# FFN up projection: four pairs of chunks by Strassen's algorithm, with sums of weight quarters made by accumulating DMA transfers

## The chip, the cores and the metric

The kernel runs on one NeuronCore of a Trainium2 chip. The engines are TensorE (PE: matmuls, into PSUM banks), VectorE (DVE), ScalarE (ACT), GpSimd (POOL) and SyncE (SP), which issues most DMA transfers. Each engine works through its own queue in order; 16 DMA engines serve all the queues that issue transfers. The metric is the time of one execution on the device in microseconds (us), as the median of several runs.

## The reference

Two layers of a decoder trunk over 256 tokens and 1024 channels, all in float32. Each layer has two half-step FFNs, one before and one after a mixer of three kinds of attention, and then a gated input embedding:

```python
def swiglu(x, w1, w3, w2):
    return (jax.nn.silu(x @ w1) * (x @ w3)) @ w2
...
    for i in range(DEPTH):
        h = h + 0.5 * swiglu(rms_norm(h, g_ffn1[i]), w1_a[i], w3_a[i], w2_a[i])
        u = rms_norm(h, g_mix[i])
        h = h + hybrid_mixer(u, w_in[i], ...)
        h = h + 0.5 * swiglu(rms_norm(h, g_ffn2[i]), w1_b[i], w3_b[i], w2_b[i])
        ple_gate = jax.nn.sigmoid(rms_norm(h, g_ple[i]) @ w_ple_gate[i])
        h = h + ple_gate * (p[i] @ w_ple_proj[i])
    return rms_norm(h, g_final)
```

The change touches only the FFNs, of which there are four. The hidden width is 2816.

## The kernel before

**Precision.** TensorE multiplies in the format fp32r. To keep float32 accuracy each operand is split into a rounded part `hi` (a cast on ScalarE) and a remainder `lo` (a subtraction on VectorE), and each product is three matmuls (`mm3`, lines 101 to 104: hi x hi, hi x lo, lo x hi). One such matmul has a 128x128 stationary part and a 128x512 moving part, which is the weights.

**Chunks of the up projection.** The hidden width is cut into 11 chunks of 256. A chunk has 512 columns: 256 of `w1` and 256 of `w3`. The 1024 rows of its weights come in four units of 128x1024 (512 KB each). A plain chunk is, for two blocks of 128 tokens and eight blocks of 128 rows, three matmuls each: 2 x 8 x 3 = 48. A plain unit (`up_unit`, line 222) loads one of the four units (`load`, line 75: a transfer on SP's queue, a cast, a remainder) and gives 12 matmuls. `gated` (line 234) makes silu(a) * b from the result, `turn` (243) transposes it with four TensorE transposes and splits it, and `down_unit` (260) loads 512 KB of `w2` and adds 12 matmuls to four PSUM banks that hold the down projection.

**Pairs.** Two chunks together are a product of 2 x 2 blocks: token blocks by halves of the rows for x, halves of the rows by chunks for the weights. Strassen's algorithm, in Winograd's form, makes it with seven products of 12 matmuls instead of eight, 84 instead of 96 for two chunks. Each product takes a sum or a quarter of the weights and a sum or a quarter of x. `x_forms` (267) makes those of x once per FFN. `winograd` (311) fetches the eight units of a pair's quarters; `form` (323) makes four sums of quarters on VectorE, two units each (line 320); `make` (335) splits the two units that a product needs, into the buffers `whi` and `wlo`, of which there are seven each for all weights; `products` (348) issues the seven products and the sums of their results. The matmuls of two products that follow one another may add to one bank, with a copy or sum taken out of it between.

**Order.** Per FFN the chunks 0 to 6 are plain and (7, 8) and (9, 10) are pairs. Chunks 0 to 2 come first. Then `block` (line 384) runs a pair: eight steps, each with the splits for the next product, a product, a plain unit of chunks 3 to 6, and a down unit. What the code says is not yet the order on the engines: the framework's planner simulates the program with assumed durations when it is built, reorders the instructions of each engine by that, and puts in the semaphore waits. After that each queue is fixed. The last chunks' down units, the residual sum into `h` and the next norm end the FFN.

Of the kernel before, what the change touches and what calls it, by code (L numbers as in the profile page):

```python
# [14 lines left out]
P = 128  # L15
# [18 lines left out]
def trunk(ctx: ExitStack, tc: tile.TileContext, a: dict, out: bass.AP):  # L34
# [77 lines left out]
    def bank_tr():  # L112
        return bank("tr", 2)
# [77 lines left out]
    def ffn(li, w13, w2, r, g, first=False, aside=None):  # L191
        nonlocal ident
        with tc.tile_pool(name=nm("fp"), bufs=3) as fp:

            def wtile():
                return fp.tile([P, U], F32, tag="wr", name=nm("wr"), bufs=10)

            def t512(name):
                return fp.tile([P, 512], F32, tag="t512", name=nm(name), bufs=4)
# [67 lines left out]
            def x_forms():  # L267
# [31 lines left out]
                V.tensor_tensor(out=s1, in0=a10, in1=a11, op=ALU.add)  # L299
# [5 lines left out]
                sub(a01, a01, s1)  # L305
# [5 lines left out]
            def winograd(c, fx):  # L311
                ws, t2s, fw = [], [], {}
                for u in range(2):
                    ws.append({(kh, nh): wtile() for kh in range(2) for nh in range(2)})
                for kh, nh in ((0, 0), (1, 0), (0, 1), (1, 1)):
                    for u in range(2):
                        nc.sync.dma_start(ws[u][kh, nh], w13[li, c + nh, 2 * kh + u])

                def sub(out, a, b):
                    V.tensor_tensor(out=out, in0=a, in1=b, op=ALU.subtract)  # L320
# [23 lines left out]
                def add(out, a, b):  # L344
                    V.tensor_tensor(out=out, in0=a, in1=b, op=ALU.add)


                def products():
                    o = bank_tr()
# [7 lines left out]
                    o = bank_tr()  # L357
                    product(o, 6, True)
                    u2 = t512("u2")
                    add(u2, o, m1)  # L360
# [758 lines left out]
```

## Time and profile before

| | us |
|---|---|
| median of 3 runs (lowest, highest) | 1333.01 (1332.68, 1333.23) |
| the profiled execution: its time | 1332.86 |
| its span in the trace | 1331.1 |
| TensorE busy, in the span | 1312.2 |
| VectorE / ScalarE busy | 994.0 / 802.8 |
| second FFN (first layer), about | 448 to 634 |

The page's first part gives busy time and share of the span by engine, the second 40 equal slices, the fourth the chain of work that ended last. A row of a group reads: line, engine, operation, output <- inputs, shapes, count | busy us, mean ns of one | idle time of the engine before these instructions, and which instruction ended it. `whi<-raw` and `wlo<-raw` are the two halves of a split of a plain load, `whi<-wr` and `wlo<-wr` those of a pair's unit; `wr<-wr,wr` are the sums of quarters; `tr`, `mm` and `acc` are PSUM banks. A row of the timeline gives start, duration and count. A row of the view of stretches gives the stretch, its length, busy time (and instructions) of each engine, TensorE's granted clock, the mean busy share of the DMA engines, and GB/s.

### The profile page before, as it was taken

How to read it: one execution, taken by the hardware profiler on the slowest of the kernel's cores; microseconds unless marked ns; L12 is line 12 of the kernel's file. 1: busy time of each engine (PE TensorE's matmuls, PEld its weight loads, DVE VectorE, ACT ScalarE, POOL GpSimd, SP SyncE). 2: the span in 40 equal slices, each digit the busy share in tenths (PEclk: the TensorE clock that was granted, in tenths of full speed). 3: DMA queues.
4: the chain of work that ended last, by engine and by line, in shares of the span. 5: the costliest groups of instructions: out<-in, count | busy, mean ns of one | idle time of the engine just before them, and what ended most of it. 6: DMA issues, size and time to landing. Idle time of an engine off the chain costs nothing.

```text
span 1331.1 us, 17969 instructions
## 1 busy us (share of the span) xinstructions
PE 1312.2 (99%) x6624; PEld 1097.5 (82%) x6624; DVE 994.0 (75%) x1414; ACT 802.8 (60%) x1205; POOL 50.2 (4%) x109
## 2 busy tenths in 40 slices
PE   9999999999999999999999999999999999999997
PEld 7788879978888888887888888898888788888876
DVE  7998755666768789975789986566676677999755
ACT  6665546665775655654756665466667835655645
POOL 1000000001100000000100000000010000000001
PEclk9999999999999999999999999999999999999999
DMA  8774537534455567455566646373444465583542
GB/s 296 274 269 127 187 103 228 171 123 132 147 169 175 161 227 276 122 164 182 163 239 196 217 128 210 103 224 127 159 142 143 144 204 167 206 299 102 180 145 80
DMA packets 67769, 236.63 MB, mean 178 GB/s; under 512 B 8160, under 2 KB 8800, under 8 KB 67680
## 3 DMA queue, kind: packets, MB, share of 16 engines
q1 hardware_dynamic: 67104, 234.39, 54.0%
q8 instruction: 52, 0.85, 0.3%
q10 hardware_dynamic: 576, 1.08, 0.2%
q14 instruction: 37, 0.30, 0.1%
HBM read 234.40 MB, written 1.05 MB: 177 GB/s over the span
## 4 chain that ended last, share of the span: by engine, by line
PE 94%; ACT 2%; DVE 2%; DMA 1%; issue 1%; POOL 0%; SPq 0%; POOLq 0%; ACTq 0%; DVEq 0%
PE mm L102 17%; PE mm L104 17%; PE mm L103 17%; PE acc L102 8%; PE acc L103 8%; PE acc L104 8%; PE tr L104 4%; PE tr L102 4%; PE tr L103 4%; PE tr L250 1%; PE tr L150 1%; ACT whi L86 1%; PE tr L716 1%; DVE wlo L87 1%; DMA h<-in_x 1%
## 5 line engine op out<-in xcount | busy, mean ns | idle before, releaser
L87 DVE TENSOR_TENSOR wlo<-raw,whi 128x1024 fp32r<-128x1024 f32 (+1 forms) x378 | 450.1, 1201 | 137.3 <-ACT whi L86 135.1
L86 ACT CAST whi<-raw 128x1024 fp32r<-128x1024 f32 (+1 forms) x378 | 387.3, 1035 | 198.2 <-PE mm L104 77.5
L102 PE MATMUL mm<-whi,xhi 128*128 128x512 f32 (+1 forms) x760 | 296.0, 393 | 0.0
L103 PE MATMUL mm<-wlo,xhi 128*128 128x512 f32 (+1 forms) x760 | 295.1, 389 | 0.3 <-DVE wlo L87 0.3
L104 PE MATMUL mm<-whi,xlo 128*128 128x512 f32 (+1 forms) x760 | 295.2, 389 | 0.0
L102 PEld LDWEIGHTS mm<-whi,xhi 128*128 128x128 f32 x760 | 143.0, 188 | 30.0 <-DVE sqk L516 0.7
L104 PEld LDWEIGHTS mm<-whi,xlo 128*128 128x128 f32 x760 | 142.8, 188 | 29.7 <-DVE xlo L136 0.7
L103 PEld LDWEIGHTS mm<-wlo,xhi 128*128 128x128 f32 x760 | 142.9, 188 | 28.9 <-DVE wlo L87 0.8
L135 ACT CAST whi<-wr 128x1024 fp32r<-128x1024 f32 (+1 forms) x120 | 121.6, 1023 | 66.9 <-PE acc L104 38.9
L136 DVE TENSOR_TENSOR wlo<-wr,whi 128x1024 fp32r<-128x1024 f32 (+1 forms) x120 | 140.6, 1185 | 24.8 <-ACT whi L135 23.6
L102 PE MATMUL acc<-whi,fhi 128*128 128x512 f32 x352 | 132.0, 393 | 7.7 <-ACT fhi L135 7.7
L103 PE MATMUL acc<-wlo,fhi 128*128 128x512 f32 x352 | 137.9, 392 | 0.4 <-DVE wlo L87 0.4
L104 PE MATMUL acc<-whi,flo 128*128 128x512 f32 x352 | 134.6, 390 | 0.0
L102 PEld LDWEIGHTS acc<-whi,fhi 128*128 128x128 f32 x352 | 65.7, 188 | 23.2 <-ACT fhi L135 9.6
L103 PEld LDWEIGHTS acc<-wlo,fhi 128*128 128x128 f32 x352 | 66.1, 188 | 15.2 <-DVE wlo L87 1.8
L104 PEld LDWEIGHTS acc<-whi,flo 128*128 128x128 f32 x352 | 66.1, 188 | 13.6
L320 DVE TENSOR_TENSOR wr<-wr,wr 128x1024 f32<-128x1024 f32 x64 | 76.3, 1217 | 0.0
L102 PE MATMUL mm<-xhi,whi 128*128 128x256 f32 x256 | 73.8, 288 | 0.0
L104 PE MATMUL mm<-xhi,wlo 128*128 128x256 f32 x256 | 72.5, 283 | 0.0
L103 PE MATMUL mm<-xlo,whi 128*128 128x256 f32 x256 | 72.4, 283 | 0.0
L102 PE MATMUL tr<-whi,q 128*128 128x512 f32 x160 | 63.7, 398 | 0.0
L104 PE MATMUL tr<-whi,q 128*128 128x512 f32 x160 | 62.6, 391 | 0.0
(248 smaller groups left out, 1960.8 us busy)
## 6 DMA issues: line engine op xcount, KB each, us to landing
raw<-in_w13b SPq DMA_DIRECT2D x56, 512.0 KB, 3.7
raw<-in_w13a SPq DMA_DIRECT2D x52, 512.0 KB, 4.2
raw<-in_wg SPq DMA_DIRECT2D x48, 512.0 KB, 3.7
raw<-in_w2a SPq DMA_DIRECT2D x44, 512.0 KB, 4.4
raw<-in_w2b SPq DMA_DIRECT2D x44, 512.0 KB, 4.3
wr<-in_w13a SPq DMA_DIRECT2D x32, 512.0 KB, 6.7
raw<-in_wqk SPq DMA_DIRECT2D x32, 512.0 KB, 4.1
wr<-in_w13b SPq DMA_DIRECT2D x32, 512.0 KB, 6.2
```

The lines of the kernel that those rows point to most:

```text
L86: A.copy(hi[:, c], raw[:, c])
L87: V.tensor_tensor(out=lo[:, c], in0=raw[:, c], in1=hi[:, c].bitcast(F32), op=ALU.subtract)
L102: PE.matmul(o, lhs[0], rhs[0], start=first, stop=False, **more)
L103: PE.matmul(o, lhs[0], rhs[1], start=False, stop=False, **more)
L104: PE.matmul(o, lhs[1], rhs[0], start=False, stop=last, **more)
L135: A.copy(hi, t)
L136: V.tensor_tensor(out=lo, in0=t, in1=hi.bitcast(F32), op=ALU.subtract)
L150: PE.transpose(t[:, j * P : (j + 1) * P], h[tb][:, k * P : (k + 1) * P], ident)
L250: PE.transpose(t[:, j * S + tb * P : j * S + (tb + 1) * P], prs[c, tb][:, j * P : (j + 1) * P], ident)
L320: V.tensor_tensor(out=out, in0=a, in1=b, op=ALU.subtract)
L716: PE.transpose(t[:, j * P : (j + 1) * P], e[:, j * P : (j + 1) * P], ident)
```

## The change

Chunks 0 to 2 stay plain, and (3, 4), (5, 6), (7, 8) and (9, 10) are pairs. A pair has four tiles x, y, w and z of two units each. The sums of quarters are no longer made on VectorE: with the signs of x's forms changed, every sum of the weights is a running sum of quarters, and `plus` adds a further quarter to a tile in SBUF by a DMA transfer with `accum_op=add`, issued from POOL's queue, after the tile's last split. Tile w is b01 + b00 for product 5, then + b11 for product 6, then + b10 for product 4; tile z is b11 for product 3, then + b01 for product 7. The products run in the order 1, 2, 5, 3, 6, 7, 4. The results of 5 and 3 are copied out by ScalarE and combined later. The order of products (S), plain units (P), down units (D) and transposes (T) stands in four plans; the quarters of the next pair are fetched one tile at a time from the third S on, and the three later pairs use the other two PSUM banks (`mm`).

```diff
             def wtile():
-                return fp.tile([P, U], F32, tag="wr", name=nm("wr"), bufs=10)
+                return fp.tile([P, U], F32, tag="wr", name=nm("wr"), bufs=12)

             def t512(name):
-                return fp.tile([P, 512], F32, tag="t512", name=nm(name), bufs=4)
+                return fp.tile([P, 512], F32, tag="t512", name=nm(name), bufs=5)
...
-                V.tensor_tensor(out=s1, in0=a10, in1=a11, op=ALU.add)
+                sub(s1, a10, a11)
...
-                sub(a01, a01, s1)
+                V.tensor_tensor(out=a01, in0=a01, in1=s1, op=ALU.add)
...
-            def winograd(c, fx):
...
-                for kh, nh in ((0, 0), (1, 0), (0, 1), (1, 1)):
+            ORDER = (1, 2, 5, 3, 6, 7, 4)
+
+            def pair(c, bank):
+                def at(kh, nh, u):
+                    return w13[li, c + nh, 2 * kh + u]
+
+                t = {q: [wtile() for _ in range(2)] for q in "xywz"}
+                fw = {}
+                quarters = {"x": (0, 0), "y": (1, 0), "w": (0, 1), "z": (1, 1)}
+
+                def fetch(q):
                     for u in range(2):
-                        nc.sync.dma_start(ws[u][kh, nh], w13[li, c + nh, 2 * kh + u])
...
-                def form(i):
-                    for u, w in enumerate(ws):
-                        if i == 1:
-                            sub(w[0, 0], w[0, 1], w[0, 0])
-                        elif i == 2:
-                            t2s.append(wtile())
-                            sub(t2s[u], w[1, 1], w[0, 0])
-                        elif i == 3:
-                            sub(w[0, 1], w[1, 1], w[0, 1])
-                        else:
-                            sub(w[1, 0], w[1, 0], t2s[u])
+                        nc.sync.dma_start(t[q][u], at(*quarters[q], u))
+
+                def plus(q, kh, nh):
+                    for u in range(2):
+                        nc.gpsimd.dma_start(t[q][u], at(kh, nh, u), accum_op=ALU.add)

                 def make(i):
-                    at = {1: (0, 0), 2: (1, 0), 7: (0, 1), 5: (0, 0), 3: (1, 1), 4: (1, 0)}
-                    fw[i] = [split_w(t2s[u] if i == 6 else w[at[i]]) for u, w in enumerate(ws)]
+                    q = {1: "x", 2: "y", 5: "w", 3: "z", 6: "w", 7: "z", 4: "w"}[i]
+                    fw[i] = [split_w(w) for w in t[q]]
+                    if i == 5:
+                        plus("w", 1, 1)
+                    elif i == 3:
+                        plus("z", 0, 1)
+                    elif i == 6:
+                        plus("w", 1, 0)
...
                 def products():
-                    o = bank_tr()
+                    o = bank()
                     product(o, 1, True)
                     m1 = t512("m1")
                     A.copy(m1, o)
                     yield
                     product(o, 2)
                     gated(c, 0, o, r[0])
                     yield
+                    o = bank()
+                    product(o, 5, True)
+                    c5 = t512("c5")
+                    A.copy(c5, o)
+                    yield
+                    product(o, 3)
+                    v = t512("v")
+                    A.copy(v, o)
+                    yield
+                    o = bank()
                     product(o, 6, True)
                     u2 = t512("u2")
+                    sum_(u2, o, m1)
+                    sum_(v, v, u2, ALU.subtract)
+                    gated(c + 1, 0, v, r[0])
                     yield
                     product(o, 7)
+                    sum_(m1, o, m1)
+                    sum_(c5, c5, m1, ALU.subtract)
+                    gated(c + 1, 1, c5, r[0])
                     yield
+                    o = bank()
                     product(o, 4, True)
+                    sum_(m1, o, m1)
                     gated(c, 1, m1, r[0])
                     yield

+                def first_sum():
+                    plus("w", 0, 0)
...
+            def block(now, plan, then=None):
+                make, _, _, ps = now
                 following = None
+                k = 0
+                for kind, *arg in plan:
+                    if kind == "S":
+                        if k < 6:
+                            make(ORDER[k + 1])
+                        if then is not None:
+                            if k == 2:
+                                following = pair(*then)
+                                following[1]("w")
+                            elif k == 3:
+                                following[1]("x")
+                                following[2]()
+                            elif k == 4:
+                                following[1]("y")
+                            elif k == 5:
+                                following[1]("z")
+                            elif k == 6:
+                                following[0](1)
                         next(ps)
+                        k += 1
+                    elif kind == "P":
...
+                        up_unit(*arg, os)
+                    elif kind == "D":
+                        down_unit(*arg)
+                    else:
+                        turn(*arg)
                 return following

-            for c in range(3):
+            for c in range(2):
...
-                    wg = winograd(7, fx)
+                    wg = pair(3, bank_tr)
+                    for q in "wxyz":
+                        wg[1](q)
+                    wg[2]()
...
+            wg = block(wg, [
+                ("S",), ("P", 2, 0), ("S",), ("D", 0, 0), ("P", 2, 1), ("S",), ("D", 0, 1), ("P", 2, 2),
+                ("T", 1), ("S",), ("P", 2, 3), ("S",), ("D", 1, 0), ("S",), ("D", 1, 1), ("S",),
+            ], (5, bank_mm))
+            wg = block(wg, [
+                ("S",), ("T", 2), ("T", 4), ("D", 2, 0), ("S",), ("S",), ("T", 3), ("D", 2, 1), ("D", 4, 0),
+                ("S",), ("S",), ("D", 4, 1), ("D", 3, 0), ("S",), ("S",),
+            ], (7, bank_mm))
...
+            wg = block(wg, [
+                ("S",), ("T", 6), ("D", 3, 1), ("S",), ("S",), ("T", 5), ("D", 6, 0), ("S",), ("S",),
+                ("D", 6, 1), ("S",), ("S",), ("D", 5, 0),
+            ], (9, bank_mm))
+            wg = block(wg, [
+                ("S",), ("T", 8), ("D", 5, 1), ("S",), ("S",), ("T", 7), ("D", 8, 0), ("S",), ("S",),
+                ("D", 8, 1), ("S",), ("S",), ("T", 10),
+            ])
+            block((None, None, None, iter(())), [
+                ("D", 7, 0), ("T", 9), ("D", 7, 1),
+            ])
```

More of the change, by code (lines that the diff above doesn't have):

```diff
@@ L342, in product, with sum_ @@
                         mm3(o, [y[:, kt, :] for y in fx[i]], m, start and kt == 0, kt == 3, skip_group_check=True)
-                def add(out, a, b):
-                    V.tensor_tensor(out=out, in0=a, in1=b, op=ALU.add)
+                def sum_(out, a, b, op=ALU.add):
+                    V.tensor_tensor(out=out, in0=a, in1=b, op=op)
                 def products():
-                    o = bank_tr()
+                    o = bank()
                     product(o, 1, True)
@@ L361, in products @@
+                    sum_(v, v, u2, ALU.subtract)
+                    gated(c + 1, 0, v, r[0])
                     yield
                     product(o, 7)
-                    add(m1, o, m1)
+                    sum_(m1, o, m1)
+                    sum_(c5, c5, m1, ALU.subtract)
+                    gated(c + 1, 1, c5, r[0])
                     yield
-                    o = bank_tr()
-                    product(o, 5, True)
-                    c22 = t512("c22")
-                    add(c22, o, m1)
@@ L369, in products @@
-                    gated(c + 1, 1, c22, r[0])
-                    yield
-                    product(o, 3)
-                    add(u2, o, u2)
-                    gated(c + 1, 0, u2, r[0])
-                    yield
-                    o = bank_tr()
+                    o = bank()
                     product(o, 4, True)
-                    add(m1, o, m1)
+                    sum_(m1, o, m1)
                     gated(c, 1, m1, r[0])
                     yield
-                return make, form, products()
@@ L384, in block @@
-            def block(wg, plain, turns, downs, then=None):
-                make, form, ps = wg
+                def first_sum():
+                    plus("w", 0, 0)
+                return make, fetch, first_sum, products()
+            def block(now, plan, then=None):
+                make, _, _, ps = now
                 following = None
                 os = []
-                for k in range(8):
-                    if k < 6:
-                        make((2, 6, 7, 5, 3, 4)[k])
-                    if k < 3:
-                        form(k + 2)
-                    if k == 6 and then is not None:
-                        following = winograd(then, fx)
-                    if k == 7 and then is not None:
-                        following[0](1)
-                        following[1](1)
-                    if k < 7:
-                        next(ps)
-                    if k % 4 == 0:
-                        os = []
-                    up_unit(plain[k // 4], k % 4, os)
-                    if k in downs:
-                        down_unit(*downs[k])
-                    for t in turns.get(k, ()):
-                        turn(t)
+                k = 0
[16 more added lines that the diff above has]
+                                following[0](1)
+                        next(ps)
+                        k += 1
+                    elif kind == "P":
+                        if arg[1] == 0:
+                            os = []
+                        up_unit(*arg, os)
[3 more added lines that the diff above has]
+                        turn(*arg)
```

25 lines of the change are left out of this document (removed).

## The prediction, made before the changed kernel was run

> **What bounds the kernel now.** I read the head of the page first: which engine is full, at what clock, and what the chain of waits runs through.
>
> ```profile
> span 1331.1 us, 17969 instructions
> ...
> PE 1312.2 (99%) x6624; PEld 1097.5 (82%) x6624; DVE 994.0 (75%) x1414; ACT 802.8 (60%) x1205; POOL 50.2 (4%) x109
> ...
> PEclk9999999999999999999999999999999999999999
> ...
> PE 94%; ACT 2%; DVE 2%; DMA 1%; issue 1%; POOL 0%; SPq 0%; POOLq 0%; ACTq 0%; DVEq 0%
> ```
>
> TensorE is busy for 99% of the span at full clock, and 94% of the chain that ended last is TensorE. A matmul that goes away is therefore worth its time, as long as nothing else becomes late. Next the FFNs by themselves: the view of stretches for the whole second FFN (448 to 634 us) and for two pieces of it.
>
> ```profile
> core 0: us, PE busy (x) PEld busy (x) DVE busy (x) ACT busy (x) POOL busy (x), PEclk, DMA share, GB/s
> 448.00:634.00 186.00, 184.07 (x841) 151.70 (x840) 149.11 (x168) 106.19 (x133) 3.21 (x8) 1.00 0.58 190
> ...
> 480.00:520.00 40.00, 40.00 (x181) 32.83 (x180) 39.77 (x42) 25.99 (x32) 0.00 (x0) 1.00 0.67 231
> ...
> 476.00:484.00 8.00, 8.00 (x38) 6.63 (x37) 7.73 (x13) 4.31 (x10) 0.00 (x0) 1.00 1.02 411
> ```
>
> Three things are to be seen. TensorE idles 2 us of 186. From 480 to 520 VectorE is busy 39.77 of 40 us and TensorE still loses nothing, so a nearly full VectorE is bearable. The DMA engines are half used over the FFN (190 GB/s), but where the eight quarters of a pair are fetched in a row they are full, at 411 GB/s. That is the ceiling I use: a 512 KB transfer takes 0.524 MB / 411 GB/s = 1.28 us of all engines.
>
> The price of a matmul comes from TensorE's timeline, where the pitch counts and not the 0.39 us shown, since matmuls overlap:
>
> ```profile
> 518.15 0.39 PE L102 MATMUL tr<-whi,q 128*128 128x512 f32 x1
> ...
> 520.88 0.39 PE L102 MATMUL mm<-whi,xhi 128*128 128x512 f32 x1
> ...
> 523.60 0.39 PE L102 MATMUL acc<-whi,fhi 128*128 128x512 f32 x1
> ```
>
> A Strassen product (12 matmuls) runs from 518.15 to 520.88, a plain unit (12 as well) from there to 523.60: 2.72 us a unit, 0.227 us a matmul.
>
> **The change part by part.**
>
> *Matmuls.* Two plain chunks are 2 x 48 = 96 matmuls, a pair is 7 x 12 = 84. Two more pairs in each of four FFNs remove 4 x 24 = 96 matmuls: 96 x 0.227 = 21.8 us off the bounding engine. This term is sure.
>
> *ScalarE and VectorE.* Per FFN the groups are:
>
> ```profile
> L87 DVE TENSOR_TENSOR wlo<-raw,whi 128x1024 fp32r<-128x1024 f32 x50 | 60.7, 1221 | 19.5 <-ACT whi L86 19.1
> L136 DVE TENSOR_TENSOR wlo<-wr,whi 128x1024 fp32r<-128x1024 f32 x28 | 33.8, 1220 | 6.2 <-ACT whi L135 5.9
> L320 DVE TENSOR_TENSOR wr<-wr,wr 128x1024 f32<-128x1024 f32 x16 | 19.1, 1217 | 0.0
> L136 DVE TENSOR_TENSOR flo<-tr,fhi 128x512 fp32r<-128x512 f32 x11 | 7.4, 683 | 0.0
> L238 DVE SCALAR_TENSOR_TENSOR pr<-mm,r,act 128x256 f32<-128x256 f32 x14 | 6.7, 481 | 5.9 <-ACT act L236 5.5
> L345 DVE TENSOR_TENSOR m<-tr,m 128x512 f32<-128x512 f32 x4 | 2.7, 683 | 0.0
> ...
> L135 ACT CAST whi<-wr 128x1024 fp32r<-128x1024 f32 x28 | 29.1, 1052 | 15.4 <-PE acc L104 9.9 <-PE tr L104 2.3 <-DVE wr L320 1.4
> ...
> L352 ACT COPY m<-tr 128x512 f32<-128x512 f32 x2 | 1.2, 589 | 4.2 <-PE tr L104 4.2
> ```
>
> VectorE loses the 16 sums of L320 (19.5 us) and 16 remainders of plain units (16 x 1.22 = 19.5), and gains 28 remainders of products (34.2) and ten more sums on results (five a pair, 10 x 0.68 = 6.8): +2 us on 149. ScalarE loses 16 casts, gains 28 (+12.6) and ten copies of results (three a pair instead of one, 10 x 0.59 = 5.9): +18.5 on 106. Neither fills the 180.6 us that an FFN would then take. The densest piece is the third of the four plans (7 products, 4 down units, 2 turns). A turn's four transposes take 0.36 us:
>
> ```profile
> 475.68 0.60 PE L250 MATMUL tr<-ident,pr 128*128 128x128 f32 x4
> 476.04 0.47 PE L102 MATMUL mm<-whi,xhi 128*128 128x512 f32 x1
> ...
> 514.66 2.35 DVE L136 TENSOR_TENSOR wlo<-wr,whi 128x1024 fp32r<-128x1024 f32 x2
> ```
>
> TensorE needs 11 x 2.72 + 2 x 0.36 = 30.6 us. VectorE, with 2.35 / 2 = 1.17 us per remainder in a row, needs 18 x 1.17 + 5 x 0.68 + 4 x 0.48 + 2 x 0.68 = 27.7 us, or 90%; the piece at 99% above bears that. I cost all of this at nothing. TensorE's own work hides it; were that cover gone, the third and fourth plans would follow VectorE.
>
> *The x forms* keep their number of operations; only signs change. Two more buffers for quarters remove this wait of the DMA queue of SP, which has cost TensorE nothing so far (first row; the other two are waits of TensorE itself, its largest and one for a copy out of a bank):
>
> ```profile
> SPq L317 <- DVE q L136: 17.9, 4, 4.8
> ...
> PE acc L102 <- ACT fhi L135: 7.7, 8, 1.2
> ...
> PE tr L102 <- ACT m L352: 0.6, 1, 0.6
> ```
>
> *The accumulating transfers.* Each pair gets eight, of 512 KB, from POOL's queue, which the page shows at 4% of the span; what waits behind them there are only the norms' few scalars after the plans. The trace of before has no such transfer. The nearest rows are the loads:
>
> ```profile
> raw<-in_w13b SPq DMA_DIRECT2D x56, 512.0 KB, 3.7
> ...
> wr<-in_w13b SPq DMA_DIRECT2D x32, 512.0 KB, 6.2
> ...
> DMA to landing us min/median/max: 4.5/6.4/9.9
> ```
>
> A load lands 3.7 us after issue when it comes alone and 6.2 in a series of fetches (the last row, all quarters of all FFNs, has 9.9 as the worst). For engine time, the lower end is a load's 1.28 us: as many bytes are written, so a gain is excluded. An accumulation must also read what it adds to. With that read beside the others, at a third pass where a load has two, it is 1.5 x 1.28 = 1.9 us; if reads alone are the limit, 2.55; if three passes run one after the other, each at a load's whole price, 3.8. I take 1.9, since the load is the nearest row and one pass is added to its two.
>
> *Volume.* The four plans hold (loads + accumulations) 16 + 8, 13 + 8, 12 + 8 and some 5 + 6, against TensorE's 41.2, 33.7, 30.6 and 28.3 us (15, 12, 11 and 10 units with 1, 3, 2 and 3 turns). At 1.9 us they need 35.7, 31.8, 30.6 and 17.8 us: it just fits, with nothing to spare in the third. At 2.55 they need 40.9, 37.0, 35.8 and 21.7: 3.3 and 5.2 us late after the second and third, less 0.3 spare in the first.
>
> *The new chain.* A tile w serves products 5, 6 and 4 in turn: split, accumulate, split, accumulate, split. A split is a cast and a remainder, 1.05 + 1.22 = 2.3 us, so the chain takes 6.9 us + 2T, T being the time from a freed tile to its landed sum. In the third plan TensorE takes six units and a turn, 16.7 us, from product 5 to product 4. Added to that is the head start of the splits: with seven buffers (two per product, one per down unit) product 5's can begin when product 1 starts, 8.5 us ahead; that splits do run as far ahead as buffers let them is in the cast's row, whose idle time ends mostly with TensorE. With the whole head start T may be 9.1 us, with half of it 7; beyond this every us costs two per pair. The first two plans have 25 and 22 us where the third has 16.7. While ScalarE waits for w, the casts for z and for the down units queue behind it, and VectorE behind them; their order is fixed when the program is built, by durations that the planner assumes, and the trace can't show what it assumes for an accumulation. T alone is 3.7 + 0.6 + 1.9 (second tile) = 6.2 us, and with the 2.5 us that a series adds, 8.7: inside the limits on the one reading, over the half one by 1.7 on the other. I take 0.5 us per pair in the third and fourth plans, 8 x 0.5 = 4 us (ends: 0, and 8 x 2 x 1.7 = 27).
>
> *The first FFN* starts with empty buffers; its stretch from 30 to 60 us moves 302 GB/s already, and 1.3 us of TensorE are idle in it:
>
> ```profile
> 30.00:60.00 30.00, 28.70 (x127) 22.69 (x126) 29.11 (x36) 19.91 (x27) 0.00 (x0) 1.00 0.82 302
> ```
>
> The sums on VectorE leave it (up to 1.3 gained), and the first pair comes a chunk (48 matmuls, 10.9 us) earlier, with 10 transfers to wait for. I take 1.5 us lost, between -1.3 and +6.
>
> *Sum.* The profiled execution took 1332.86 us (span 1331.1 and 1.8 around it), 0.15 below the median 1333.01. 1332.9 - 21.8 + 4 + 1.5 = **1316.6 us**, 1.2% faster.
>
> **The Trainium skill on the disputed price.** The Trainium skill, "Collectives: The Full Stack", section "The bandwidth ceiling: the fold count and why AG ≠ RS ≠ AR", says that a reducing transfer is slower because it reads two sources through the same ring, not because of the add, and gives 32.35 against 62.28 GB/s. By that ratio, 1.93, an accumulation here would be an estimated 2.5 us, which speaks against this change; no run here shows it yet. It weighs in the chance of the first rival.
>
> **The rivals.**
>
> 1. *Reads bind: 2.55 us.* The third plan's DMA work (35.8 us) exceeds TensorE's time. By volume each FFN is 8.2 us late. By the chain, T is 3.7 + 1.3 + 2.55 = 7.5 us alone, and with loads taking half of full engines 2.4 + 4 x 2.55 = 12.6 (2.4 is 3.7 less its own 1.28), 3.5 us over the full limit, 7 per pair in two plans. The two delays overlap; I take 8 to 15 us per FFN: 1332.9 - 21.8 + 4 x (8 to 15) = 1343 to 1371, middle **1355**: slower. It decides from about 5.4 us per FFN on. For it: the full engines at 476 to 484. Against: the mean of 190 GB/s leaves room elsewhere.
> 2. *Three passes in a row: 3.8 us.* Plans need 50.9, 47.0, 45.8 and 29.2 us: 9.7 + 13.3 + 15.2 + 0.9 = 39 us late per FFN, 1332.9 - 21.8 + 156 = **1467**. Nothing in the trace speaks for it, nothing excludes it.
> 3. *Banks.* Products 5 and 3, 6 and 7, and 1 and 2 share a bank, with a copy or sum between; where one unit instead of two lies between them and VectorE has a queue, TensorE waits. 0.5 us at 3 places of 16 pairs is 24 us: **1335**, no change. Against it: one such wait of 0.6 us in the whole run before.
>
> **How the numbers follow.** Chances: forecast 0.50, first rival 0.35, second 0.06, third 0.09. The forecast's own range is 1309 to 1329 (all hidden; or 13 us more stalls). About 0.2%, 2.7 us, can be told from no change here. Faster: the forecast, 0.50. Same: nearly all of the third, 0.08. Slower: both first rivals and the rest, 0.42. For eight in ten the range takes in the first rival up to 1368 and leaves the second out: 1309 to 1368.
>
> **What would show it.** Right: 2976 instead of 3072 up and down matmuls, busy TensorE some 21 us shorter, FFNs of 181 to 183 us, casts waiting for TensorE and not for DMA. The first rival: casts of w waiting for DMA from POOL, TensorE idle in the third and fourth plans, DMA share near 1.0 there. The third: products waiting for ScalarE's copy or VectorE's sums. The prediction is wrong if an accumulation lands later than about 9 us, or the engines deliver fewer than 340 GB/s of source bytes (20 x 0.524 MB in 30.6 us) in the third plan.

## The result, and the profile after

The changed kernel takes **1458.36 us** (median of 3 runs, 1455.68 to 1460.36) against 1333.01 before: a ratio of 1.094 with an interval of 1.091 to 1.097. It is slower by 125 us, where 16 us of gain were forecast and the range ended at 1368. The profiled execution took 1455.68 us, with a span of 1453.7. Medians and ratios here and below leave out one run far from all others: 2632 us, in the version with three pairs and all sums by DMA.

The head of the page of the changed kernel, with the DMA queue of the accumulating transfers (packets, MB, share of 16 engines' span) and the chain that ended last:

```profile
span 1453.7 us, 18287 instructions
...
PE 1338.5 (92%) x6528; PEld 1102.3 (76%) x6528; DVE 1002.0 (69%) x1438; ACT 862.6 (59%) x1293; POOL 160.3 (11%) x237
...
PEclk9889999999999988999989999999999999989999
...
q0 software_dynamic: 18432, 67.12, 23.8%
...
PE 31%; DMA 11%; issue 8%; DVE 5%; ACT 1%; POOL 1%; POOLq 0%; ACTq 0%; DVEq 0%
```

The 96 matmuls are gone (6528 against 6624), and yet TensorE is busy 26 us longer and idle 115 us instead of 19. The chain, 94% TensorE before, now goes 11% through DMA (only about half of it is named). Queue q0 holds the 128 accumulating transfers: 23.8% of 1453.7 us is 346 us of all engines, 2.70 us for each, where 1.9 had been taken. (The same transfers without the add, in a version below, have 13.6% of 1351.9 us on that queue, 1.44 us each.)

The same FFN as in the prediction, which now lies at 482 to 696 us, as a whole and in stretches of 10 us:

```profile
core 0: us, PE busy (x) PEld busy (x) DVE busy (x) ACT busy (x) POOL busy (x), PEclk, DMA share, GB/s
482.00:696.00 214.00, 188.26 (x810) 150.79 (x809) 150.45 (x173) 120.92 (x155) 30.76 (x40) 0.94 0.86 243
...
502.00:512.00 10.00, 8.26 (x40) 6.73 (x38) 2.34 (x5) 1.69 (x4) 1.83 (x2) 1.00 1.02 329
512.00:522.00 10.00, 3.20 (x7) 2.21 (x8) 9.89 (x14) 7.46 (x10) 0.00 (x0) 0.53 0.75 227
...
542.00:552.00 10.00, 7.38 (x35) 5.77 (x33) 2.73 (x3) 3.63 (x5) 0.00 (x0) 1.00 1.05 276
552.00:562.00 10.00, 7.33 (x24) 5.55 (x24) 3.51 (x6) 3.29 (x6) 0.00 (x0) 0.83 1.04 314
562.00:572.00 10.00, 7.03 (x19) 5.60 (x20) 8.51 (x10) 5.37 (x6) 1.72 (x2) 0.66 1.04 365
572.00:582.00 10.00, 10.00 (x48) 8.07 (x48) 8.90 (x12) 7.31 (x10) 2.62 (x3) 1.00 1.05 339
...
622.00:632.00 10.00, 7.50 (x29) 5.78 (x29) 4.81 (x6) 5.48 (x8) 1.72 (x2) 0.83 1.04 225
```

There are two kinds of loss. At 502 to 522 TensorE loses 8.5 us, and DMA does not fill the engines at its end: that is before the pairs begin. From 542 to 572 it loses some 3 us of 10 with the DMA engines full (1.04 to 1.05); until 562 VectorE and ScalarE are idle for about two thirds of the time as well, so neither is at its limit. But full engines alone don't stall TensorE: from 572 to 602 they are as full (1.05) and it loses nothing. After the stalls the granted clock falls, to 0.53 and 0.66 in the rows at 512 and 562; idle time and low clock together leave 19 matmuls in the 10 us from 562, in place of some 45.

The waits of TensorE and of ScalarE in the changed kernel (us in total, times, longest):

```profile
PE tr L102 <- ACT whi L135: 32.3, 4, 8.1
PE tr L102 <- DVE u L346: 20.2, 4, 5.3
PE mm L102 <- ACT c L361: 17.2, 8, 4.4
PE tr L102 <- DVE flo L136: 13.5, 4, 4.0
...
ACT whi L135 <- DMA wr<-in_w13b: 67.9, 37, 6.1
ACT whi L135 <- DMA wr<-in_w13a: 66.1, 39, 5.2
```

ScalarE waits 134 us for the tiles of pairs, where before its casts waited mostly for TensorE. These tiles are filled by fetches (SP's queue) and changed by accumulations (POOL's queue), and the view by source line tells the two apart. Who waited for the accumulations (us, times), and who for the fetches:

```profile
  ACT whi L135: 133.4, 75
```

```profile
  ACT whi L135: 0.6, 1
```

So it is the sums that ScalarE waits for, although the fetches land late too. TensorE does not wait for DMA itself: it waits for whatever stands behind those casts, copies out of banks (`c`), sums of results (`u`), remainders of a turn (`flo`). And the first row is one wait of 8.1 us in each of the four FFNs. The DMA issues, the last number being the median from issue to landing:

```profile
wr<-in_w13a SPq DMA_DIRECT2D x64, 512.0 KB, 9.1
wr<-in_w13a POOLq DMA_DIRECT2D x64, 512.0 KB, 10.0
wr<-in_w13b SPq DMA_DIRECT2D x64, 512.0 KB, 8.3
wr<-in_w13b POOLq DMA_DIRECT2D x64, 512.0 KB, 9.5
```

Fetches of quarters, at a median of 6.2 and 6.7 us before, land after 8.3 to 9.1 us, the accumulations after 9.5 to 10.0.

### The profile page after: what moved, and what is told of

Same layout as the page of the kernel before. It is cut to its first block, busy times and chain, and to the rows that moved or that the text cites. A ratio compares the mean times of both kernels' runs of the same rounds, so it can differ in the third digit from the quotient of the medians.

```text
span 1453.7 us, 18287 instructions
## 1 busy us (share of the span) xinstructions
PE 1338.5 (92%) x6528; PEld 1102.3 (76%) x6528; DVE 1002.0 (69%) x1438; ACT 862.6 (59%) x1293; POOL 160.3 (11%) x237
## 3 DMA queue, kind: packets, MB, share of 16 engines
q0 software_dynamic: 18432, 67.12, 23.8%
HBM read 301.50 MB, written 1.05 MB: 208 GB/s over the span
## 4 chain that ended last, share of the span: by engine, by line
PE 31%; DMA 11%; issue 8%; DVE 5%; ACT 1%; POOL 1%; POOLq 0%; ACTq 0%; DVEq 0%
PE mm L102 7%; PE mm L104 6%; PE mm L103 6%; DMA wr<-in_w13b 5%; DMA wr<-in_w13a 5%; PE acc L104 2%; PE acc L103 2%; PE acc L102 2%; DVE wlo L136 2%; ACT whi L135 1%; DVE wlo L87 1%; PE tr L150 1%; POOL wr L328 1%; DVE q L136 0%; PE tr L737 0%
## 5 line engine op out<-in xcount | busy, mean ns | idle before, releaser
L87 DVE TENSOR_TENSOR wlo<-raw,whi 128x1024 fp32r<-128x1024 f32 (+1 forms) x314 | 372.1, 1197 | 99.9 <-ACT whi L86 96.8
L86 ACT CAST whi<-raw 128x1024 fp32r<-128x1024 f32 (+1 forms) x314 | 318.9, 1029 | 139.6 <-PE mm L104 39.0
L136 DVE TENSOR_TENSOR wlo<-wr,whi 128x1024 fp32r<-128x1024 f32 (+1 forms) x232 | 276.1, 1203 | 160.9 <-ACT whi L135 158.5
L135 ACT CAST whi<-wr 128x1024 fp32r<-128x1024 f32 (+1 forms) x232 | 235.3, 1033 | 176.8 <-DMA wr<-in_w13b 67.9
L102 PE MATMUL mm<-whi,xhi 128*128 128x512 f32 (+1 forms) x600 | 235.9, 395 | 4.7 <-ACT whi L86 2.3
L103 PE MATMUL mm<-wlo,xhi 128*128 128x512 f32 (+1 forms) x600 | 233.1, 389 | 0.8 <-DVE wlo L87 0.8
L104 PE MATMUL mm<-whi,xlo 128*128 128x512 f32 (+1 forms) x600 | 233.1, 389 | 0.0
L103 PEld LDWEIGHTS mm<-wlo,xhi 128*128 128x128 f32 x600 | 112.8, 188 | 23.4 <-DVE wlo L87 1.1
L102 PE MATMUL mm<-whi,q 128*128 128x512 f32 x240 | 101.1, 421 | 28.3 <-ACT c L361 17.2
L103 PE MATMUL mm<-wlo,q 128*128 128x512 f32 x240 | 98.3, 410 | 0.0
L104 PE MATMUL mm<-whi,q 128*128 128x512 f32 x240 | 98.0, 409 | 0.0
L328 POOL DMA_DIRECT2D wr<-in_w13a x64 | 56.1, 898 | 280.2 <-DVE wlo L136 117.8
```

The lines of the kernel that those rows point to most:

```text
L86: A.copy(hi[:, c], raw[:, c])
L87: V.tensor_tensor(out=lo[:, c], in0=raw[:, c], in1=hi[:, c].bitcast(F32), op=ALU.subtract)
L102: PE.matmul(o, lhs[0], rhs[0], start=first, stop=False, **more)
L103: PE.matmul(o, lhs[0], rhs[1], start=False, stop=False, **more)
L104: PE.matmul(o, lhs[1], rhs[0], start=False, stop=last, **more)
L135: A.copy(hi, t)
```

## The experiments

The theories at the start: D, the accumulations are the cause; A, POOL's queue; B, the denser plans; C, three passes in a row; F, VectorE. To these came the stall ahead of the pairs, with the forms of x as its suspect.

**What one accumulation costs, by itself.** The kernel before, with four bursts of twelve 512 KB transfers behind its end:

```diff
+        for i, t in enumerate(T):
+            nc.sync.dma_start(t, src(i))
+        join()
+        for i, t in enumerate(T):
+            nc.gpsimd.dma_start(t, src(i + 12))
+        join()
+        for i, t in enumerate(T):
+            nc.gpsimd.dma_start(t, src(i), accum_op=ALU.add)
+        join()
...
```

> The kernel before with four bursts of twelve 512 KB transfers behind its end, with nothing else on the DMA engines: plain from SP, plain from POOL, accumulating from POOL, and six plain from SP mixed with six accumulating from POOL (this adds a tail and changes nothing of the output). Theory: plain bursts move 400 to 415 GB/s from either queue (1.28 us each), the accumulating one 195 to 225 GB/s (2.3 to 2.7 us each), as two reads for one write would give; the mixed one 6 x 1.28 + 6 x 2.5 = 23 us. Rival A (POOL's queue is the price): the plain POOL burst is as slow as the accumulating one. Rival C (three passes one after another): 130 to 140 GB/s, 3.8 us each.

VectorE adds 16 columns of each tile as it lands, so its timeline shows the landings (start, duration, instruction, and in brackets the idle time before); first plain transfers from SP, then accumulating ones from POOL:

```profile
1344.15 0.18 DVE L1044 TENSOR_TENSOR bs<-bs,b 128x16 f32<-128x16 f32 x1 [1.07 <-DMA b<-in_w13a]
...
1352.88 0.18 DVE L1044 TENSOR_TENSOR bs<-bs,b 128x16 f32<-128x16 f32 x1 [1.06 <-DMA b<-in_w13a]
...
1388.89 0.18 DVE L1044 TENSOR_TENSOR bs<-bs,b 128x16 f32<-128x16 f32 x1 [2.02 <-DMA b<-in_w13a]
...
1406.31 0.18 DVE L1044 TENSOR_TENSOR bs<-bs,b 128x16 f32<-128x16 f32 x1 [2.30 <-DMA b<-in_w13a]
```

Seven pitches from 1344.15 to 1352.88 make 1.25 us a load, 420 GB/s. Seven from 1388.89 to 1406.31 make 2.49 us an accumulation, 211 GB/s of source. The plain transfers from POOL's queue land in between, the first and the last of them at

```profile
1358.05 0.17 DVE L1044 TENSOR_TENSOR bs<-bs,b 128x16 f32<-128x16 f32 x1 [3.94 <-DMA b<-in_w13a]
...
1372.29 0.18 DVE L1044 TENSOR_TENSOR bs<-bs,b 128x16 f32<-128x16 f32 x1 [1.06 <-DMA b<-in_w13a]
```

which is 1.29 us in the mean of 11 pitches. The price is the add's, not the queue's, and it is twice a load: the first rival's 2.55, neither 1.9 nor 3.8. In the mixed burst the twelve landings lie between 1410.44 and 1433.21, 22.8 us, near the 23 expected.

**The adds taken away, and the forms of x moved.** In the first kernel the transfers of the changed kernel stay where they are and only lose their add; the order on every queue is identical. In the second the forms of x are issued a chunk earlier in the second to fourth FFN; the third has both edits.

```diff
-                        nc.gpsimd.dma_start(t[q][u], at(kh, nh, u), accum_op=ALU.add)
+                        nc.gpsimd.dma_start(t[q][u], at(kh, nh, u))
...
+                if c == 1 and not first:
+                    fx = x_forms()
...
-                    fx = x_forms()
+                    if first:
+                        fx = x_forms()
```

> The changed kernel with the add taken out of its 128 transfers: the same bytes from the same queue at the same places, with every queue in the same order, but they overwrite the tile instead of adding (so the products get quarters where sums belong). Theory: of the 34 us per FFN that the changed kernel lies behind its matmul count, about 20 are the price of the add (2.7 us of all DMA engines per 512 KB in its trace, at full engines), about 10 the start of the pairs. Then the time falls by some 80 us, to 1365 to 1385, and the engines' share per POOL transfer falls from 2.7 to under 1.8 us. Rival A (POOL's software queue: 0.87 us to issue one, late waits): unchanged, above 1440. Rival B (the dense plans themselves, without regard to DMA): above 1420.

> The changed kernel with the x forms issued one chunk earlier in the second to fourth FFN (in the first the norm's scale isn't there yet). Theory: TensorE's stall of 8 us and the low clock behind it at the first product of these FFNs go away, 3 x 8 to 10 us: 1428 to 1436. Rival D (the accumulations are the only bound, so that work done earlier waits later): 1450 to 1460.

> Both edits: no add, and the x forms a chunk earlier in three FFNs. Theory: the two costs add up and little else is wrong with four pairs: 1333 - 22 + 10 (start of the first FFN) + 10 to 25 for late transfers of 1.3 us: 1330 to 1350. Rival B (dense plans): above 1390.

| | adds | plain |
|---|---|---|
| forms as changed | 1458.4 | 1354.05, ratio 1.016 (1.013 to 1.018) |
| forms a chunk earlier | 1436.5, ratio 1.077 (1.074 to 1.080) | 1326.4, ratio 0.996 (0.993 to 0.999) |

The adds cost 104 us with late forms and 110 with early ones, more than the 80 expected; both plain versions came out below their expected ranges. POOL's queue, the plans, VectorE and the denser chain of products are all still there in the version at 1326.4, so A, B and F do not explain the slowness. (POOL needs less time to issue a plain transfer; a run below with the long issue and half the bytes settles that part of A.) The place of the forms costs 22 to 28 us. The planner builds the same order with and without the adds; what duration it assumes for an add the runs do not show.

Where the forms stood in the way is in ScalarE's timeline of the changed kernel, and in the row of TensorE that waits:

```profile
510.01 0.26 ACT L276 COPY rb<-tr 128x128 f32<-128x128 f32 x1
...
515.16 2.18 ACT L135 CAST q<-wr 128x512 fp32r<-128x512 f32 x4 [1.48 <-DVE wr L284]
517.24 3.88 ACT L135 CAST whi<-wr 128x1024 fp32r<-128x1024 f32 x4
```

```profile
518.34 0.80 PE L102 MATMUL tr<-whi,xhi 128*128 128x512 f32 x1 [8.08 <-ACT whi L135]
```

The casts of the forms (`q`) depend on a small matmul behind chunk 1, whose result is copied to `rb`, and on VectorE's sums of x; the pair's first split stands behind them on ScalarE. With three plain chunks ahead, as in the kernel before, that time lay under chunk 2.

**Volume or chain.** The adds could delay TensorE by filling the engines, so that every load beside them lands late (theory V), or because they are made in place, so that a split waits for the sum that it needs and ScalarE's queue with it (theory K). For this the transfers were turned aside: from the version with early forms, same size, same queue, behind the same split, but into side tiles that nobody reads. Buffers for quarters go from 12 to 10 for room.

```diff
-                        nc.gpsimd.dma_start(t[q][u], at(kh, nh, u), accum_op=ALU.add)
+                        d = sides[u]
+                        nc.gpsimd.tensor_copy(d[:, :8], (src or t[q])[u][:, :8])
+                        nc.gpsimd.dma_start(d, at(kh, nh, u), accum_op=ALU.add)
```

> The changed kernel with the forms of x a chunk earlier, in which every accumulating transfer keeps its size, its queue and its place behind the same split, but adds into one of two side tiles that nobody reads (the products take the quarters unsummed, so the result is another). To make room, the quarters have 10 buffers instead of 12. The volume stays, the chain split, sum, split is gone. The version with the chain took 1436.5, the one without the adds 1326.4. Theory V, by volume: loads and fetches land late beside full engines whoever reads the sums, so most of the 110 us stay: 1390 to 1440. Theory K, by the chain in place: the waits of ScalarE for a sum from POOL's queue were most of it: 1325 to 1350.

> The control of the kernel with side tiles: the same instructions in the same order on every queue, the transfers into the side tiles plain instead of accumulating. Both theories: 1320 to 1335, as the version with plain transfers into the tiles themselves (1326.4). What this run takes less than the one with accumulating side transfers is the price of the adds by volume alone: theory V 60 us or more, theory K below 25.

With the adds this kernel took 1388.2 us (1.042, 1.040 to 1.044), its control with plain transfers 1320.7 (0.991, 0.989 to 0.993): 67 us, between the theories. But ScalarE's casts waited 32.6 us for POOL's small copy, which held a buffer of the splits. So the mark that keeps each transfer behind its split went over a small tile of its own (a column copied by VectorE, then by POOL):

> The kernel with side tiles again, but the mark that keeps each side transfer behind its split goes over a small tile of its own (a copy of one column by VectorE, then one by POOL), so that no buffer of the splits waits for POOL. Volume, queues and side tiles are as before; the result is another, as there. If the hold was most of the 67 us (theory K: the volume alone is nearly covered by TensorE's work): 1325 to 1350. If the loss is the volume (theory V): 1370 to 1390, and the loads land as late as in the run before.

> Its control with plain side transfers, the same order on every queue: 1318 to 1330 by both theories. The difference to the run with accumulating side transfers is the adds' price by volume alone: below 25 us by theory K, above 45 by theory V.

Now 1341.0 us (1.005, 1.003 to 1.008; ten runs from 1330.8 to 1350.3) against 1323.9 (0.993, 0.992 to 0.995): 17 us for the volume of all 128 adds. The view of stretches of f1b_aside, an FFN's middle:

```profile
500.00:560.00 60.00, 60.00 (x270) 49.14 (x269) 48.29 (x63) 40.43 (x49) 13.65 (x21) 1.00 1.05 310
```

and the same stretch of the version with sums in place and early forms:

```profile
500.00:560.00 60.00, 48.52 (x202) 38.21 (x201) 38.28 (x43) 31.14 (x39) 10.58 (x12) 0.91 1.04 322
```

The engines are as full (1.05 and 1.04), but TensorE is busy 60.00 of 60 us in one and 48.52 in the other. Nor are the fetches earlier: they land after 9.4 and 10.1 us (medians) beside the side tiles, after 8.9 and 9.3 with sums in place. So late loads are not what costs, and theory K carries most of it: about 93 of the 110 us. The comparison is not pure: with two side tiles each add waits for the one two before it, so the bursts are smoother, and buffers and order differ from the version in place; so the two shares are approximate.

**How a late sum reaches TensorE**, and whether fewer adds help. Pairs taken away (two pairs; three pairs), then, with three and four pairs, two of the four sums given back to VectorE in place, since w + x and w + z need only tiles that are there:

```diff
+                    held = {(0, 0): "x", (1, 1): "z", (1, 0): "y"}
+                    if (kh, nh) in ((0, 0), (1, 1)):
+                        for u in range(2):
+                            sum_(t[q][u], t[q][u], t[held[kh, nh]][u])
+                        return
```

> The accumulating sums alone: two pairs, (7, 8) and (9, 10), with chunks 0 to 6 plain as in the kernel before, but with the sums of quarters made by accumulating transfers and the products in the changed kernel's order. Each product has a plain unit and mostly a down unit beside it. Theory (an accumulation costs 2.5 us of the engines and is late only where the plans are dense): 66 x 1.25 + 16 x 2.5 = 123 us of DMA work in a FFN of 185, and three units per product of cover for the chain: no loss, 1328 to 1340. Rival E (a tile's split, accumulate, split chain is late wherever it stands): above 1350.

> Three pairs, (5, 6), (7, 8) and (9, 10), with accumulating sums; chunks 0 to 2 plain ahead of the pairs as in the kernel before, so that the x forms have their cover. 48 matmuls fewer than before: 10.9 us. DMA work 66 x 1.25 + 24 x 2.5 = 143 us in a FFN of 182. Theory: 1322 plus 0 to 4 us per FFN where the last plan (7 products, 7 down units) is late: 1322 to 1338. Rival E: above 1350.

> As the one before, but two of a pair's four sums (w + x and w + z, whose quarters lie in SBUF already) made by VectorE in place, so that a pair has four accumulating transfers instead of eight, and the chain of w only one. DMA work 82 + 12 x 2.5 = 112 us in 182, VectorE some 154 us busy. Theory: both engines have room, and TensorE's saving shows: 1321 to 1327, faster than both kernels. Rival E: above 1340. Rival F (the third pair costs VectorE what TensorE saves): 1330 to 1336.

> The changed kernel's four pairs and plans, with the two sums by VectorE as in the run before, the x forms a chunk earlier, and in the first FFN chunk 2 ahead of the pairs. DMA work 82 + 16 x 2.5 = 122 us in 181; VectorE needs about 136 us in the four plans, where TensorE has 134. Theory: the DMA bound is gone and VectorE is at its limit: 1311 plus 2 to 6 us per FFN, 1319 to 1335. Rival D (the accumulations bind even at half their number): above 1380.

Measured: two pairs 1374.9 (1.031, 1.029 to 1.034), three 1383.5 (1.038, 1.036 to 1.039), three with two sums by VectorE 1350.2 (1.013, 1.012 to 1.015), four so with early forms 1404.9 (1.054, 1.052 to 1.056). All four miss their theories and lie where the rivals E and D had put them: the accumulations are late in looser plans too. Even two pairs, as many as before, lose 42 us. No plain control stands beside these versions and their plans differ, so they show that the loss stays, not what one sum costs. A single stall per FFN is left in the three-pair kernel with mixed sums, and there it can be followed. POOL's queue and then ScalarE's:

```profile
509.92 0.87 POOL L333 DMA_DIRECT2D wr<-in_w13b  x1 [0.21 <-issue]
```

```profile
521.88 1.04 ACT L135 CAST whi<-wr 128x1024 fp32r<-128x1024 f32 x1 [2.73 <-DMA wr<-in_w13b]
522.84 0.58 ACT L370 COPY v<-tr 128x512 f32<-128x512 f32 x1
523.31 1.05 ACT L86 CAST whi<-raw 128x1024 fp32r<-128x1024 f32 x1
524.26 0.84 ACT L236 ACTIVATE act<-mm,r 128x256 f32<-128x256 f32 x2
```

The accumulation issued at 509.92 is awaited until 521.8, 11.9 us. Behind the cast wait a copy of a result, a cast of a down unit and the activation of a plain chunk, which frees a bank; the wait that TensorE shows for it is that of the bank's product (`pr`):

```profile
PE mm L102 <- DVE pr L238: 22.3, 4, 5.9
```

> The changed kernel with each accumulation cut to the first 512 of 1024 columns: 128 transfers as before, each with 256 KB of source, so about the engine time of a plain one of 512 KB (the other half of each sum is left out). Theory G (what is paid is the doubled bytes, by engine time and landing): like the run without the add, 1345 to 1370. Rival H (a fixed price per accumulating transfer: its issue of 0.87 us, its descriptors): above 1410.

> The kernel with the x forms a chunk earlier (1436.5 us), where now the splits for products 6, 7 and 4 stand right before their own product and not one product ahead. Accumulations and their bytes stay. Theory I (a late sum costs what queues behind its cast on ScalarE, since the order there is fixed for a sum that lands in about 6 us): less stands behind it, 1385 to 1420. Rival J (the engines' volume is the bound, whatever the order): 1428 to 1445.

Accumulating only 512 of the 1024 columns in the changed kernel gives 1362.1 (1.022, 1.020 to 1.024): half the bytes take away 96 of the 104 us. So the cost in these plans goes by the bytes and not by a fixed price per transfer, and not in proportion: the loss sets in past a point. POOL is as busy there as in the changed kernel (160.8 us against 160.3), so its longer issue of an add is not the price either. Splitting for the products 6, 7 and 4 right before they are needed, so that less stands behind a waiting cast, gives 1461.3 (1.096, 1.093 to 1.100) against 1436.5 with early splits: slower, outside both ranges expected. The probable reason, not shown: in a chain of split, sum, split, a later split makes the next sum later too.

**What the plan is worth without the chain.** Three pairs, early forms, chunk 2 in the plans, three sums by VectorE in place (w + x, w + z, w + y) and only z + b01 by DMA, with the split for product 7 late. Beside it z = w - x by VectorE as well, no accumulation at all; the first with its one transfer plain; and four pairs in this manner.

```diff
-                    if (kh, nh) in ((0, 0), (1, 1)):
+                    if (kh, nh) in ((0, 0), (1, 1), (1, 0)):
...
-                        if k < 6:
+                        late = (7,)
+                        if k < 6 and ORDER[k + 1] not in late:
...
+                        if ORDER[k] in late:
+                            make(ORDER[k])
```

> A version meant to beat both: three pairs, (5, 6), (7, 8) and (9, 10); x forms a chunk earlier, chunk 2 among the first plan's units (ahead of it in the first FFN); three of the four sums of a pair made by VectorE in place (w + x, w + z, w + y), and only z + b01 by an accumulation, with three products between its issue and its use; its split stands right before product 7. 48 matmuls fewer than before, 10.9 us. Theory: two accumulations per pair with 16 us of cover cost nothing, VectorE has 132 of 147 us in the plans: 1321 to 1328. Rival E (an accumulation is late wherever it stands): above 1335.

> The same three pairs without any accumulating transfer: z is made by VectorE as well, as w - x after w + z. VectorE has 139 of 147 us in the plans. Theory: still room, 1322 to 1330, close to the run beside it. Rival F (VectorE at 95% delays products): 1330 to 1340.

> The fastest version so far (three pairs, three sums in place by VectorE, only z + b01 by an accumulating transfer: 1317.12 us) with this one transfer plain, so that b01 replaces b11 instead of being added (another result); the order on every queue is the same. If two accumulations per pair, with room before the product that needs them, are covered by TensorE's work: 1316 to 1318. If each costs its extra 1.25 us of the engines on the path, 24 of them: 1287 to 1300.

> Four pairs like the changed kernel, but three of a pair's four sums by VectorE in place and only z + b01 by an accumulating transfer, its split late, the forms of x a chunk earlier and chunk 2 ahead in the first FFN. TensorE saves four more times 12 matmuls against the three-pair version (10.9 us); VectorE gets 8 more sums and 6 more remainders' worth of work per FFN, some 179 of 181 us. If VectorE's load is bearable: 1306 to 1315. If VectorE or the denser plans bind (theories B and F): 1317 to 1345, and the fourth pair does not pay in this form.

Measured: **1317.1** (0.988, 0.987 to 0.990) with one sum by DMA, faster than both kernels by 16 and 141 us; 1322.3 (0.992, 0.990 to 0.993) with none; 1317.4 (0.988, 0.987 to 0.990) with the transfer plain, so 24 accumulations with time in hand cost nothing that shows; and 1330.8 (0.998, 0.997 to 0.999) with four pairs. The first beat its forecast of 1321 to 1328; the last fell in the range of its theories B and F. It says something on theory K as well: from the four pairs with two sums by VectorE (1404.9) it differs in two edits alone, w + b10 made by VectorE and the late split for product 7. ScalarE's waits for accumulations go from 144.9 us to 4.6 and the time falls by 74 us, with half as many accumulating transfers (32 in place of 64) and more work on VectorE (1100.0 us against 1067.9). Two stretches of the version with four pairs at 1330.8, one in the first FFN and one in the second:

```profile
40.00:60.00 20.00, 17.00 (x74) 12.93 (x74) 20.00 (x20) 13.04 (x16) 1.97 (x2) 1.00 0.94 347
...
500.00:520.00 20.00, 20.00 (x92) 16.53 (x91) 19.75 (x22) 13.40 (x17) 0.00 (x0) 1.00 0.99 341
```

VectorE is at 19.75 to 20 of 20 us. In the second stretch TensorE bears it, in the first it loses 3 us. That VectorE takes the fourth pair's gain is possible but not shown: the DMA engines are at 0.94 in the first stretch too, and the three-pair version at 1317.1 loses 2.6 us in the same stretch, also with VectorE at 20.00.

## Why the prediction was wrong

**The accumulation's price, "1.9 us".** The step failed by size: 2.49 us in a row and 2.70 in the kernel's mean, twice the 1.25 of a load. The reasoning "one pass is added to its two" was wrong; the first rival's price holds. That "reads alone are the limit" is its explanation; no run shows which part of the transfer is the limit. The Trainium skill ("Collectives: The Full Stack", section "The bandwidth ceiling: the fold count and why AG ≠ RS ≠ AR") puts a reducing transfer among four ranks at 1.93 times a copy, because of its second source read; here the ratio is 2.49 / 1.25 = 1.99, so the trace agrees with the ratio; the reason it does not show. The prediction named this ratio and then took the smaller price.

**T and the 4 us.** T was taken as 6.2 to 8.7 us; the medians are 9.5 and 10.0 and the one followed above 11.9, past the 9.1 that the prediction set as its own limit. That alone made rival 1 the case. But rival 1's 1355 (the middle of its bounds is 1357) was too low by over 100 us, with the price and nearly the T right (it had 12.6 beside full loads). What it sized wrongly is what a late sum costs: 8 to 15 us per FFN, where 104 / 4 = 26 were measured. Three things were missing. First, the place: the loss was put into the third and fourth plans, while the trace has its longest stretch at 542 to 572, in the first. By volume the first plan had 0.3 us to spare even at 2.55; but fetches, loads and adds came in bursts with the engines at 1.05, and the lateness is made there. Second, the queue: a waiting cast was charged with its own product only, while copies, activations and turns stand behind it on ScalarE in an order that is fixed. The prediction named that queue and gave it no price. Third, the granted clock. With the same 6528 matmuls TensorE is busy 1338.5 us here and 1294.9 in the plain version with early forms: 44 of the 132 us between them are the same matmuls taking longer, at a mean granted clock of 0.960 against 0.993.

**Volume.** "By volume each FFN is 8.2 us late" was the rival's first estimate: the volume alone cost 17 / 4 = 4 us per FFN. In the stretch shown the engines are full for 60 us with TensorE losing nothing, if what is late is not awaited at once.

**The forms of x, put at nothing.** The prediction says only that they "keep their number of operations", and its sum has no term for them. That was wrong: with two plain chunks ahead instead of three, their cover is gone. I had asked for the cover of moved work at ScalarE and VectorE, but looked at how much they do, not at what stands before the first split in their queues. Price: 22 to 28 us for three FFNs; the first FFN's 8.1 us wait stays.

**The first FFN, "1.5 us lost" (end +6).** The stretch from 20 to 80 us in the kernel before, the version at 1326.4, and f1_plain:

```profile
20.00:80.00 60.00, 57.95 (x256) 46.31 (x255) 56.32 (x68) 39.03 (x54) 1.01 (x3) 1.00 0.80 284
```

```profile
20.00:80.00 60.00, 48.38 (x197) 38.02 (x196) 43.79 (x56) 36.28 (x50) 7.67 (x15) 0.89 0.95 369
```

```profile
20.00:80.00 60.00, 50.91 (x213) 40.60 (x212) 46.39 (x59) 37.98 (x51) 12.10 (x23) 0.91 0.92 345
```

The plain version with early forms issues 59 matmuls fewer there than the kernel before, f1_plain 43 fewer: at 0.227 us these are 13.4 and 9.8 us lost, beyond the end of 6.

**Right:** 96 matmuls fewer, and their 21.8 us where nothing stalls: 1332.9 - 21.8 = 1311, plus the first FFN's 13.4 or 9.8 is 1324.5 or 1320.9, and the two plain versions took 1326.4 and 1320.7 (f1b_plain, with 213 matmuls in this stretch as well, 1323.9). ScalarE's and VectorE's added work (nothing) and the two banks (rival 3) also held, since the same edits stand in those versions: the waits of TensorE in the version at 1326.4 for a sum or a copy out of a bank are small:

```profile
PE tr L102 <- ACT whi L135: 8.1, 1, 8.1
...
PE tr L102 <- DVE u L346: 2.9, 3, 2.2
PE tr L102 <- ACT m L353: 1.6, 3, 0.7
```

POOL's queue was no bound. Rival 2 fell with its price of 3.8 us; that its 1467 is near the result is chance.

The terms that failed, in short: 4 us for late sums where the adds cost 104, nothing for the forms where their place cost 28, and 1.5 us for the first FFN where 13 were lost. The sum as the runs give it: 1311 + 13 (the first FFN's start) + 2 (unnamed) + 28 (forms) + 104 (adds) = 1458.

## What to carry to other kernels

A transfer that adds in place cost two loads of the DMA engines here (2.49 us against 1.25), and beside loads it landed after 9.5 to 10.0 us in the median, at most 23.4 in the changed kernel: use it for a sum that is needed three products later, as in the version at 1317.1, and give the sums on a chain of split, sum, split to an engine that adds in place at once. A late operand costs not only its own delay but that of everything queued behind the instruction that waits for it, and here the clock fell after many of the stalls; so price a wait by that queue. When work is moved ahead, look at each engine's queue before the first instruction that needs it: its cover is what ran there, not the engine's mean load.

## What the runs showed of the hardware

The accumulation takes the DMA engines almost exactly twice as long as a load (1.99 times). Issuing one also takes POOL longer than issuing a plain one, in POOL's timeline of the bursts:

```profile
1359.75 0.54 POOL L1055 DMA_DIRECT2D b<-in_w13a  x1 [0.71 <-DVE bs L1044]
...
1381.59 0.88 POOL L1058 DMA_DIRECT2D b<-in_w13a  x1 [1.52 <-DMA b<-in_w13a]
```

The clock was not expected. TensorE's timeline of the changed kernel behind a stall of 3 us, the first number of a row being its start:

```profile
552.38 0.50 PE L102 MATMUL tr<-whi,q 128*128 128x512 f32 x1 [3.01 <-DVE flo L136]
...
553.18 0.39 PE L102 MATMUL tr<-whi,q 128*128 128x512 f32 x1
553.41 0.51 PE L103 MATMUL tr<-wlo,q 128*128 128x512 f32 x1
553.72 0.63 PE L104 MATMUL tr<-whi,q 128*128 128x512 f32 x1
554.14 0.63 PE L102 MATMUL tr<-whi,q 128*128 128x512 f32 x1
```

The pitch goes from 0.23 to 0.42 us about a microsecond after the stall has ended. The Trainium skill ("TensorE: Matmul & The Clock Gate", section "HAM oscillation — how this bites in real kernels") warns of gaps in TensorE's work above some 3.4 us. The trace does not bear that bound out: the clock fell after this gap of 3.0 us, and of two gaps of 2.5 us one was followed by a pitch of 0.43 us (from 629.05) and one by the full 0.23 (from 674.67).

Left open is how much of the 93 us of the chain comes from the order of ScalarE's queue, since no kernel kept the in-place sums and changed that order alone.
